# SwiGLU gate and up products with tokens on partitions, weight chunks split whole into rings, and a written order on four engines

## The chip, the core and the metric

The kernel runs on one core of a Trainium2 chip. The engines that matter are TensorE (PE, matrix products), VectorE (DVE), ScalarE (ACT), GpSimd (POOL) and SyncE (SP, which issues the weight transfers). The metric is the device time of the program in microseconds (us). Before the change three runs took 753.84, 753.91 and 754.42 us; the median is 753.91.

## The reference

A hybrid decoder layer on 256 tokens of width 1024, all in float32. Three sub-layers follow each other, each with an RMS norm before and after it: a SwiGLU FFN of width 2816, a mixer (a Mamba-2 branch and a differential-attention branch, merged by gates), and a second SwiGLU FFN. What the change rewrites is the gate and up part of

```python
def swiglu(x, w_gate, w_up, w_down):
    return (jax.nn.silu(x @ w_gate) * (x @ w_up)) @ w_down
```

and the handling of all weights.

## The kernel before

**Split products.** Float32 accuracy comes from three products of reduced operands. Each operand is split into hi, a rounded copy (ACT, `whi`, L167), and lo, the rest (DVE, `wlo`, L168); a product is hi x hi + lo x hi + hi x lo. Activations are split in the same way (L191, L192).

**Chunks.** All weights come from DRAM in 122 chunks of 1 MB, [128 partitions x 2048], loaded by SP into three `raw` buffers. Each chunk is split in two halves of 1024 columns; the halves lie in one pool of 29 buffers (`k4`) that other tiles share. `take` hands a chunk to the products and has the chunks split three ahead (AHEAD). Chunks 0 to 32 belong to the first FFN, 33 to 88 to the mixer, 89 and up to the second FFN.

**The FFN.** The tokens are two blocks of 128. The first 512 columns of gate and of up are done by `mm_nat` (L222): activations stationary, 512 weight columns moving, tokens on partitions; PE turns the result by transposes (`pt_f`, L551). The other 2304 columns of each are done by `mm_w` (L206): weights stationary, chunks of 1024 x 256. For each 128x128 piece of weight, hi moves 512 columns (256 tokens' hi and lo) and lo moves 256. Its result lies with the columns on partitions, which is the form that the down product needs. ACT copies one half of the sum out (L219) and DVE adds the other (L220), then come silu, the product and its split.

**The down product** (`mm_n`, L427) accumulates in four PSUM tiles, two token blocks b by two halves q of 512 columns. The last three chunks are held: block 0 is done for all three, then block 1, first the half q=0 for the three chunks, then q=1. So block 0's norm can run while block 1 is done. `turned` puts block 0's transposes for the next sub-layer (`pu`, L340) among the products of block 1.

**The norms.** After each sub-layer, per block: two square sums on ACT (`jp`, L325), the gain product on DVE (`og`, L411), the power on POOL (`rp`, L330 and L331), the residual on DVE (`h`, L420). For the next norm two square sums (`sq`, L325), the power on POOL (`r`), the scaling (`un`, L373), PE's transposes (`pu`), and the split of the turned result (`u`, L343 and L345). Block 0 goes on unscaled, and its scale comes in later; block 1 is scaled first. `Norm.products` does the first four chunks of the next sub-layer for both blocks, eight products of 12 matmuls; a table says after which product block 1 is turned (after the third, in the mixer and the second FFN).

**The order.** A scheduler sets the order of the instructions on each engine, apart from the stretches in which `own_order` takes the written order for the engines it names: all four at the start and PE alone in the tails of the two kinds of down product, up to the end of the eight products behind them. SP and POOL take their queues in order, transfers too.

Of the kernel before, what the change touches and what calls it, by code (L numbers as in the profile page):

```python
# [24 lines left out]
P = 128  # L25
# [8 lines left out]
K4_BUFS = 29  # L34
K3_BUFS = 3
K2_BUFS = 7
RAW_BUFS = 3
AHEAD = 3
# [5 lines left out]
SSD_US = 1.55  # L44
BREAK, STOP = object(), object()
# [3 lines left out]
def tile_hybrid_layer(ctx: ExitStack, tc: tile.TileContext, x, ffn1_pre_g, ffn1_w_gate, ffn1_w_up,  # L49
# [9 lines left out]

    def k4(shape, name, dt=F32):  # L60
        return sb.tile(shape, dt, tag="k4", name=name, bufs=K4_BUFS)

    def k3(shape, name, dt=F32):
        return sb.tile(shape, dt, tag="k3", name=name, bufs=K3_BUFS)
# [4 lines left out]
    def jk(shape, name):  # L69
        return sb.tile(shape, F32, tag="jk", name=name, bufs=2)  # L70
# [16 lines left out]
    chunks = []  # L87

    def t_chunk(w, k0, c0):
        chunks.append((w[k0:k0 + D, c0:c0 + T].rearrange("(j p) c -> p j c", p=P), [P, KD, T]))  # L90

    def s_chunk(w, k0, c0):
        chunks.append((w[k0:k0 + 512, c0:c0 + 512].rearrange("(j p) c -> p j c", p=P), [P, 4, 512]))

    def n_chunk(w, k0):
        chunks.append((w[k0:k0 + 2 * P, :].rearrange("(j p) c -> p j c", p=P), [P, 2, D]))
# [3 lines left out]

    def ffn_chunks(wg, wu, wd):
        for w in (wg, wu):
            for k0 in (0, 512):
                s_chunk(w[0], k0, 0)
        for j in range(2, FF // T):
            t_chunk(wg[0], 0, j * T)
            t_chunk(wu[0], 0, j * T)
        for j in range(FF // T):
            n_chunk(wd[0], j * T)

    ffn_chunks(ffn1_w_gate, ffn1_w_up, ffn1_w_down)
    for c in range(2):
        for k0 in (0, 512):
            s_chunk(w_in2, k0, V0 + c * 512)
# [9 lines left out]
    for c in range(4):  # L124
        for k0 in (0, 512):
            s_chunk(w_in2, k0, G0 + c * 512)
    for c in range(2):
        for k0 in range(0, 2 * D, 512):
            s_chunk(ssd_w_branch[0], k0, c * 512)
    for c in range(2):  # L130
        for k0 in (0, 512):
            s_chunk(da_w_branch[0], k0, c * 512)
    for c in range(4):
        n_chunk(w_out[0], c * 2 * P)
    ffn_chunks(ffn2_w_gate, ffn2_w_up, ffn2_w_down)

    raws, splits = [], []
    taken = [0]

    def load_to(n):  # L140
        while len(raws) < min(n, len(chunks)):
            i = len(raws)
            src, shape = chunks[i]
            r = sb.tile(shape, F32, tag="raw", name=f"raw{i}", bufs=RAW_BUFS)
            nj = shape[1] // 4 if i == 0 else shape[1] // 2 if i < 4 else shape[1]
            for j in range(0, shape[1], nj):
                nc.sync.dma_start(r[:, j:j + nj, :], src[:, j:j + nj, :])
            raws.append(r)

    def split_steps(ahead=True):  # L150


        i = len(splits)
        load_to(i + 1)
        r, shape = raws[i], chunks[i][1]
        nj = shape[1] // 2
        his, los = [], []
        splits.append((his, los))
        for q in range(2):
            hi = k4([P, nj, shape[2]], f"whi{i}{q}", F32R)  # L160
            lo = k4([P, nj, shape[2]], f"wlo{i}{q}", F32R)
            his.append(hi)
            los.append(lo)
            n = 1 if i == 0 else nj
            for j in range(0, nj, n):
                js = slice(j, j + n)
                nc.scalar.copy(hi[:, js, :], r[:, q * nj + j:q * nj + j + n, :])  # L167
                nc.vector.tensor_sub(lo[:, js, :], r[:, q * nj + j:q * nj + j + n, :], hi[:, js, :].bitcast(F32))  # L168
                yield
        raws[i] = None  # L170
        if ahead:
            load_to(i + 1 + RAW_BUFS)

    def split_to(n):

        while len(splits) < min(n, len(chunks)):
            for _ in split_steps():
                pass

    def take(ahead=AHEAD):  # L180
# [3 lines left out]
        split_to(i + ahead)  # L184
        his, los = splits[i]
        splits[i] = None
        nj = chunks[i][1][1] // 2
        return (lambda j: his[j // nj][:, j % nj, :], lambda j: los[j // nj][:, j % nj, :])
# [17 lines left out]
    def mm_w(dst, name, w, act):  # L206


        (wh, wl), (ah, _, ahl) = w, act
        for m in range(2):  # L210
            acc = pj(f"{name}{m}")
            cs = slice(m * P, (m + 1) * P)
            for j in range(KD):
                if j:
                    nc.tensor.matmul(acc[:, :T], wl(j)[:, cs], ah(j), start=False, stop=False)  # L215
                nc.tensor.matmul(acc, wh(j)[:, cs], ahl(j), start=j == 0, stop=j == KD - 1)  # L216
                if not j:
                    nc.tensor.matmul(acc[:, :T], wl(j)[:, cs], ah(j), start=False, stop=False)
            nc.scalar.copy(dst[:, m, :], acc[:, T:])  # L219
            nc.vector.tensor_tensor(dst[:, m, :], acc[:, :T], dst[:, m, :], ALU.add)  # L220

    def mm_nat(acc, w, act, k0, first, last, late):  # L222
# [7 lines left out]
        for i, ((a, b), j) in enumerate(terms):  # L230
            nc.tensor.matmul(acc, a(k0 + j), b(j), start=first and i == 0, stop=last and i == 11)  # L231
# [43 lines left out]
    load_to(RAW_BUFS)  # L275
# [60 lines left out]
    def turn(b, q, src, g, to, name):  # L336
# [7 lines left out]
        for i in range(4):  # L344
            nc.vector.scalar_tensor_tensor(lo[:, i, :], pu[:, i, :], g(q * 4 + i), hi[:, i, :].bitcast(F32),  # L345
                                           ALU.mult, ALU.subtract)
        return pu

# [73 lines left out]
    def load_gain(v, name):  # L422
        pg = k4([P, D], name)
# [3 lines left out]
    def mm_n(acc, acts, ready, turned, begun=lambda: None):  # L427
# [25 lines left out]
        own_order(PE)  # L453
# [4 lines left out]
        for q in range(2):  # L458
            for i, w in held:
                if q == 1 and i == n - TAIL:  # L460
                    turned()
                one(i, w, ((1, (q,)),))
        split_to(taken[0] + AHEAD)
        ready(1)

    class Norm:
# [3 lines left out]
        def __init__(self, tag, g):  # L470
# [4 lines left out]
            self.left = []  # L475

# [8 lines left out]
        def unit1(self, engs=(nc.vector, nc.vector)):  # L485
            r = rms(1, self.tag)
            self.un = [unit(1, q, r, self.tag, engs[q]) for q in range(2)]

        def turn1(self, q):
            turn(1, q, self.un[q], self.g, in_u(1), self.tag)  # L490

        def products(self, ws, evict, at, turns=((0, 0), (0, 1), (1, 0), (1, 1)), late="u"):
# [4 lines left out]
            for b, i in turns:  # L497
                act = of_block(self.to0 if b == 0 else in_u(1))
                acc = pj(f"pn_{self.tag}{b}{i}")
                for c in range(2):  # L500
                    mm_nat(acc, ws[2 * i + c], act, c * 4, c == 0, c == 1, late if b == 0 else "u")
                    n += 1
                    for f in at.get(n, ()):
                        f()
                if b == 1:
# [3 lines left out]
            free_order()  # L509
# [11 lines left out]
        def rescale(self):  # L521
            set_u(rescaled(self.pus, self.r0, self.g, self.tag, self.dr))
# [7 lines left out]
    def ffn(post_v, tag, norm, ready, turned, then, at, ws=None, **kw):  # L530
# [16 lines left out]
        def back(b):  # L547
            bs = slice(b * P, (b + 1) * P)
            pt_ = bg([P, 4, P], f"pt_{tag}{b}")
            for m in range(4):  # L550
                nc.tensor.transpose(pt_[:, m, :], sgs[b][:, m * P:(m + 1) * P], ident)  # L551
            split(gh[:, :, bs], gl[:, :, bs], pt_)

        norm.products(ws or [take(1) for _ in range(4)], evict,
                      {n: [f if f else lambda: back(0) for f in fs] for n, fs in at.items()}, **kw)
        back(1)
        del sgs
        then()
        for j in range(2, FF // T):
# [633 lines left out]
```

## Time and profile before

| what | us |
|---|---|
| median of three runs | 753.91 |
| profiled execution, its span | 753.1 |
| TensorE busy (share of the span) | 743.7 (99%) |
| VectorE busy | 521.7 (69%) |
| ScalarE busy | 440.1 (58%) |
| weights and other data read from DRAM | 136.17 MB, 182 GB/s over the span |

The profile shows one execution; its own time is the span of 753.1 us, and the median of the runs lies 0.8 us above it. In the page each row has the engine, the line, the tile that is written and those that are read, the shape and the count. A row of the chain of waits has the start, the duration and what was on the chain; consecutive instructions of a kind are one row. A row of the timeline has the start, the duration (of all instructions in it, if there are several), the instruction, and in brackets the idle time ahead of it with what ended it. A row by stretches of time has the stretch, its length, the busy time of PE, PE's weight loads, DVE, ACT and POOL with the number of instructions, the granted clock, the DMA share and GB/s. PE's matmuls are pipelined, and their durations overlap.

### The profile page before, as it was taken

How to read it: one execution, taken by the hardware profiler on the slowest of the kernel's cores; microseconds unless marked ns; L12 is line 12 of the kernel's file. 1: busy time of each engine (PE TensorE's matmuls, PEld its weight loads, DVE VectorE, ACT ScalarE, POOL GpSimd, SP SyncE). 2: the span in 40 equal slices, each digit the busy share in tenths (PEclk: the TensorE clock that was granted, in tenths of full speed). 3: DMA queues.
4: the chain of work that ended last, by engine and by line, in shares of the span. 5: the costliest groups of instructions: out<-in, count | busy, mean ns of one | idle time of the engine just before them, and what ended most of it. 6: DMA issues, size and time to landing. Idle time of an engine off the chain costs nothing.

```text
span 753.1 us, 11054 instructions
## 1 busy us (share of the span) xinstructions
PE 743.7 (99%) x4377; PEld 646.1 (86%) x4377; DVE 521.7 (69%) x792; ACT 440.1 (58%) x737; POOL 38.2 (5%) x72
## 2 busy tenths in 40 slices
PE   8999999999999999999999999999999999999996
PEld 6888888888889999898999788788888888888885
DVE  6686677654577978767778988695684867766612
ACT  7475566643565565858966556784463756565511
POOL 6400000000300000000000000000010000000000
PEclk9999999999999999999999999999999999999999
DMA  8685765587253556565555463467361776555701
GB/s 300 161 265 182 224 224 207 200 286 228 64 166 116 174 163 215 165 210 176 187 168 177 165 219 127 153 224 251 112 225 56 224 224 217 173 173 183 290 1 56
DMA packets 94212, 137.96 MB, mean 183 GB/s; under 512 B 2684, under 2 KB 68304, under 8 KB 94160
## 3 DMA queue, kind: packets, MB, share of 16 engines
q1 hardware_dynamic: 91488, 129.51, 52.5%
q0 software_dynamic: 2368, 7.22, 3.1%
q8 instruction: 34, 0.56, 0.3%
q10 hardware_dynamic: 304, 0.53, 0.2%
q14 instruction: 18, 0.15, 0.1%
HBM read 136.17 MB, written 1.08 MB: 182 GB/s over the span
## 4 chain that ended last, share of the span: by engine, by line
PE 96%; DVE 1%; DMA 1%; POOL 1%; ACT 1%; issue 0%; SPq 0%; DVEq 0%; POOLq 0%
PE acc_f L441 16%; PE pup_f L216 9%; PE pg_f L216 9%; PE pws L231 6%; PE pgt L231 6%; PE pn_f L231 5%; PE pg_f L215 4%; PE pup_f L215 4%; PE acc_mx L441 3%; PE pn_mx L231 3%; PE pwd L231 3%; PE pxs L204 2%; PE pxs L202 2%; PE pxs L201 2%; PE pz L204 2%; PE pz L201 2%
## 5 line engine op out<-in xcount | busy, mean ns | idle before, releaser
L168 DVE TENSOR_TENSOR wlo<-raw,whi 128x1024 fp32r<-128x1024 f32 (+1 forms) x246 | 291.6, 1214 | 56.3 <-ACT whi L167 53.6
L167 ACT CAST whi<-raw 128x1024 fp32r<-128x1024 f32 (+1 forms) x246 | 247.3, 1044 | 59.9 <-PE acc_f L441 21.8
L216 PE MATMUL pg_f<-u_f,whi 128*128 128x512 f32 x288 | 101.2, 396 | 0.0
L216 PE MATMUL pup_f<-u_f,whi 128*128 128x512 f32 x288 | 101.1, 396 | 0.0
L215 PE MATMUL pg_f<-u_f,wlo 128*128 128x256 f32 x252 | 70.5, 280 | 0.0
L215 PE MATMUL pup_f<-u_f,wlo 128*128 128x256 f32 x252 | 70.3, 279 | 0.0
L216 PEld LDWEIGHTS pg_f<-u_f,whi 128*128 128x128 f32 x288 | 52.9, 188 | 9.7
L216 PEld LDWEIGHTS pup_f<-u_f,whi 128*128 128x128 f32 x288 | 52.7, 188 | 9.8
L441 PE MATMUL acc_f<-whi,gh_f 128*128 128x512 f32 x176 | 58.2, 390 | 0.0
L441 PE MATMUL acc_f<-wlo,gh_f 128*128 128x512 f32 x176 | 58.1, 389 | 0.0
L441 PE MATMUL acc_f<-whi,gl_f 128*128 128x512 f32 x176 | 58.1, 389 | 0.0
L215 PEld LDWEIGHTS pg_f<-u_f,wlo 128*128 128x128 f32 x252 | 47.5, 188 | 1.7
L215 PEld LDWEIGHTS pup_f<-u_f,wlo 128*128 128x128 f32 x252 | 47.5, 189 | 1.6
L220 DVE TENSOR_TENSOR su_f<-pup_f,su_f 128x256 f32<-128x256 f32 x36 | 15.2, 423 | 38.7 <-ACT su_f L219 38.7
L441 PEld LDWEIGHTS acc_f<-whi,gl_f 128*128 128x128 f32 x176 | 33.0, 188 | 6.9
L441 PEld LDWEIGHTS acc_f<-wlo,gh_f 128*128 128x128 f32 x176 | 33.0, 188 | 6.8
L441 PEld LDWEIGHTS acc_f<-whi,gh_f 128*128 128x128 f32 x176 | 33.0, 188 | 6.8
L231 PE MATMUL pgt<-whi,u_mx 128*128 128x512 f32 x128 | 34.8, 400 | 0.0
L201 PE MATMUL pz<-u_mx,whi 128*128 128x256 f32 x128 | 32.3, 288 | 0.0
L202 PE MATMUL pz<-u_mx,whi 128*128 128x256 f32 x128 | 31.8, 284 | 0.0
L201 PE MATMUL pxs<-u_mx,whi 128*128 128x256 f32 x128 | 31.7, 285 | 0.0
L202 PE MATMUL pxs<-u_mx,whi 128*128 128x256 f32 x128 | 31.4, 283 | 0.0
(318 smaller groups left out, 1425.9 us busy)
## 6 DMA issues: line engine op xcount, KB each, us to landing
raw<-in_w_in_dram SPq DMA_DIRECT2D x40, 1024.0 KB, 5.4
raw<-in_ffn_w_down_dram SPq DMA_DIRECT2D x22, 1024.0 KB, 5.3
raw<-in_ffn_w_gate_dram SPq DMA_DIRECT2D x20, 1024.0 KB, 5.7
raw<-in_ffn_w_up_dram SPq DMA_DIRECT2D x20, 1024.0 KB, 6.1
raw<-in_ssd_w_branch_dram SPq DMA_DIRECT2D x8, 1024.0 KB, 5.0
acb<-acd POOLq DMA_DIRECT2D x8, 512.0 KB, 4.9
raw<-in_da_w_branch_dram SPq DMA_DIRECT2D x4, 1024.0 KB, 5.1
raw<-in_w_out_dram SPq DMA_DIRECT2D x4, 1024.0 KB, 4.9
```

The source lines that it names most:

```text
L167: nc.scalar.copy(hi[:, js, :], r[:, q * nj + j:q * nj + j + n, :])
L168: nc.vector.tensor_sub(lo[:, js, :], r[:, q * nj + j:q * nj + j + n, :], hi[:, js, :].bitcast(F32))
L201: nc.tensor.matmul(acc[m], wh(j)[:, cs], ah(k0 + j), start=first and j == ks[0], stop=False)
L202: nc.tensor.matmul(acc[m], wh(j)[:, cs], al(k0 + j), start=False, stop=False)
L204: nc.tensor.matmul(acc[m], wl(j)[:, cs], ah(k0 + j), start=False, stop=last and j == ks[-1])
L215: nc.tensor.matmul(acc[:, :T], wl(j)[:, cs], ah(j), start=False, stop=False)
L216: nc.tensor.matmul(acc, wh(j)[:, cs], ahl(j), start=j == 0, stop=j == KD - 1)
L220: nc.vector.tensor_tensor(dst[:, m, :], acc[:, :T], dst[:, m, :], ALU.add)
L231: nc.tensor.matmul(acc, a(k0 + j), b(j), start=first and i == 0, stop=last and i == 11)
L441: nc.tensor.matmul(acc[b][q], x_[:, ts], w_(kt)[:, halves[q]], start=i == 0 and kt == 0 and x_ is ah and w_ is wh, stop=i == n - 1 and kt ...
```

## The change

1. The 2304 columns of gate and of up that `mm_w` did are now done by `mm_nat`, in groups (GROUPS = "hnnnn"): one half group, whose chunks hold 256 gate and 256 up columns, and four groups of 512. Gate, up, silu and product have tokens on partitions; each result of a block is turned by two or four transposes (`turned_back`), four products later (TURN), and split from PSUM. The code has a further form of group ("s") with functions of its own that GROUPS doesn't choose.
2. A chunk is split by one cast and one subtraction of 2048 columns. Hi and lo have rings of three buffers, one more in the FFNs; `raw` has three, two more in the FFNs. The first two chunks of the mixer and of the second FFN are still split in halves, into `k4`, and the first chunks of all in pieces. `k4` and other tiles come from a pool of the stage (first FFN, mixer, second FFN); a new stage's pool takes the space of the one that was closed.
3. PE, ACT, DVE and SP take the written order in the FFNs' products and from the held chunks of a down product to the end of the eight products behind it. In it, `prepare_to` writes the splits: two chunks ahead before the held blocks, the third and a further cast before block 1's post norm (`ready(1)`), the fourth between block 1's square sums and `un` (`unit1`). Block 1 of the held chunks is done chunk by chunk, both halves together, and block 0's transposes come ahead of the last chunk.
4. The mixer's masks (`m3`, `after_m`, `dneg`) lie in the mixer's pool; the gain of the first post norm is loaded earlier; two small tiles move to `k2`.

```diff
-    def mm_w(dst, name, w, act):
...
+MIX_K4 = 20
+FFN_K4 = 11
+RAW_MORE = 2
+SPLIT_BUFS = 3
+SPLIT_MORE = 1
+TURN = 4
...
+    def ring(kind, n, more, name, c, dt=F32):
+        i = rings.get(kind, 0) % (n + more)
+        rings[kind] = rings.get(kind, 0) + 1
+        if i < n or stage[1][1] != FFN_K4 or mixing(c):
+            return sb.tile([P, 2 * D], dt, tag=kind, name=name, bufs=n)
+        return stage[1][0].tile([P, 2 * D], dt, tag=kind, name=name, bufs=more)
...
+    def cast_next():
+        if not todo and begun[0] < len(uses):
+            more_ops()
+        if todo and todo[0].act:
+            todo[0].act()
+            todo[0].act = None
...
+    def prepare_to(n):
+        while prepared[0] < min(n, len(uses)):
+            next_op()
...
-        own_order(PE)
+        own_order(PE, ACT, DVE, SP)
+        prepare_to(taken[0] + 2)
         for q in range(2):
             for i, w in held:
                 one(i, w, ((0, (q,)),))
         ready(0)
-        for q in range(2):
-            for i, w in held:
-                if q == 1 and i == n - TAIL:
-                    turned()
-                one(i, w, ((1, (q,)),))
-        split_to(taken[0] + AHEAD)
+        while held:
+            if len(held) == 1:
+                turned()
+            one(*held.pop(0), ((1, (0, 1)),))
+        prepare_to(taken[0] + 3)
+        cast_next()
         ready(1)
...
         def unit1(self, engs=(nc.vector, nc.vector)):
             r = rms(1, self.tag)
+            prepare_to(taken[0] + 4)
             self.un = [unit(1, q, r, self.tag, engs[q]) for q in range(2)]
...
+        def turned_back(gu_, b, hi, lo):
+            m = gu_.shape[1] // P
             bs = slice(b * P, (b + 1) * P)
+            pt_ = bg([P, m, P], f"pt_{tag}{slot[0]}")
+            for i in range(m):
+                nc.tensor.transpose(pt_[:, i, :], gu_[:, i * P:(i + 1) * P], ident)
+            split(hi[:, :, bs], lo[:, :, bs], pt_)
+
+        def product(acc, w, f, k0, first, last, go_on=False, now=None, then=None):
+            for d in [d for d in due if d[0] <= slot[0]]:
+                due.remove(d)
+                d[1]()
+            mm_nat(acc, w, f, k0, first, last, "w", go_on)
+            if now:
+                now()
+            pace()
+            if then:
+                then()
+            slot[0] += 1
+
+        def two(name, evict_):
+            accs = [pj(f"{name}{b}") for b in range(2)]
+            for c in range(2):
+                w = take(1)
+                for b in range(2):
+                    product(accs[b], w, act_b[b], c * 4, c == 0, c == 1,
+                            then=(lambda: evict_(b, accs[b])) if c else None)
+
+        def plain(name, hi, lo):
+            sg = []
+
+            def gate(b, acc):
+                sg.append(k2([P, 512], f"sg_{name}{b}"))
+                act(sg[b], acc, AF.Silu)
+
+            two(f"pg_{name}", gate)
+            two(f"pu_{name}", lambda b, acc: multiplied(sg[b], acc, b, hi, lo))
...
-    m3 = const.tile([P, 3, P], F32, name="m3")
+    m3 = stage[1][0].tile([P, 3, P], F32, tag="m3", name="m3", bufs=1)
```

The first place is ACT at the seam from the first FFN to the mixer. The names: jp_f11 are the square sums of block 1, u0 and u1 the two halves of block 0's turned result, sq_mx the sums for the next norm, whi a chunk's cast. Before:

```order
L325 ACTIVATE jp_f110_1781,sp_f11_1780<-acc_f110_1342 128x512
L343 ACTIVATE u0_mx_1698<-pu_mx00_1718,cols_a_109 128x128 x4
L343 ACTIVATE u1_mx_1699<-pu_mx01_1731,cols_a_109 128x128 x4
L167 CAST whi360_1841<-raw36_1634 128x1024
L167 CAST whi361_1845<-raw36_1634 128x1024
L325 ACTIVATE jp_f111_1785,sp_f11_1780<-acc_f111_1343 128x512
```

And in the change:

```order
L509 ACTIVATE u0_mx_1386<-pu_mx00_1412,cols_a_112 128x128 x4
L509 ACTIVATE u1_mx_1387<-pu_mx01_1425,cols_a_112 128x128 x4
L491 ACTIVATE sq_mx00_1439,ss_mx0_1438<-h_72 128x512
L491 ACTIVATE sq_mx01_1441,ss_mx0_1438<-h_72 128x512
L254 CAST whi35_1458<-raw35_1312 128x2048
L254 CAST whi36_1464<-raw36_1322 128x2048
L491 ACTIVATE jp_f110_1467,sp_f11_1466<-acc_f110_1062 128x512
L491 ACTIVATE jp_f111_1471,sp_f11_1466<-acc_f111_1063 128x512
```

Block 0's square sums moved behind u, two whole casts stand ahead of jp, and both halves of jp are together.

The second place is ACT where the mixer's eight products end. v0 and v1 are the attention's values (v1 is read from pn_mx11, the last of the eight products), wdt_h is the cast of the weight that PE's next matmuls (pdt) need. Before:

```order
L674 COPY v0_1839<-pn_mx10_1927 128x512
L191 CAST u0_mx_1698<-us_mx0_1948 128x4x128
L191 CAST u1_mx_1699<-us_mx1_1953 128x4x128
L167 CAST whi390_2111<-raw39_1849 128x1024
L191 CAST wdt_h_2004<-wdt_2002 128x256
L167 CAST whi391_2115<-raw39_1849 128x1024
L674 COPY v1_1840<-pn_mx11_1975 128x512
```

And in the change:

```order
L371 CAST u1_mx_1387<-us_mx1_1637 128x4x128
L979 COPY v0_1533<-pn_mx10_1611 128x512
L979 COPY v1_1534<-pn_mx11_1659 128x512
L371 CAST wdt_h_1700<-wdt_1698 128x256
L254 CAST whi39_1787<-raw39_1490 128x2048
```

The cast of wdt moved behind v1.

The third place is ACT at the seam from the mixer to the second FFN (jp_mxp are the mixer's square sums, sq_f2 those of the second FFN's norm), in the change:

```order
L491 ACTIVATE sq_f200_5033,ss_f20_5032<-h_72 128x512
L254 CAST whi91_5052<-raw91_4907 128x2048
L491 ACTIVATE sq_f201_5035,ss_f20_5032<-h_72 128x512
L254 CAST whi92_5059<-raw92_4917 128x2048
L509 ACTIVATE u0_f2_4980<-pu_f200_5006,cols_a_112 128x128 x4
L509 ACTIVATE u1_f2_4981<-pu_f201_5019,cols_a_112 128x128 x4
L491 ACTIVATE jp_mxp10_5062,sp_mxp1_5061<-acc_mx10_4857 128x512
L254 CAST whi93_5209<-raw93_4927 128x2048
L491 ACTIVATE jp_mxp11_5066,sp_mxp1_5061<-acc_mx11_4858 128x512
```

Three whole casts stand among the norms' operations; before, block 0's and block 1's first sums stood ahead of u there, as at the first seam.

413 lines of the change are left out of this document (302 added, 111 removed).

## The prediction

> **What bounds the kernel now.** I read the page first, for who is busy; then PE's waits, for what work could be removed from in front of it; then stretches of the FFN by engine, for the price of one matmul.
>
> ```profile
> span 753.1 us, 11054 instructions
> PE 743.7 (99%) x4377; PEld 646.1 (86%) x4377; DVE 521.7 (69%) x792; ACT 440.1 (58%) x737; POOL 38.2 (5%) x72
> PEclk9999999999999999999999999999999999999999
> PE 96%; DVE 1%; DMA 1%; POOL 1%; ACT 1%; issue 0%; SPq 0%; DVEq 0%; POOLq 0%
> ```
> ```profile
> PE warm L294 <- POOL ident L280: 1.6, 1, 1.6
> PE pn_f L231 <- ACT whi L167: 0.6, 1, 0.6
> PE pu_f L340 <- POOL un_f L373: 0.5, 1, 0.5
> PE pac L739 <- DVE av L735: 0.3, 1, 0.3
> PE py L820 <- DVE E L815: 0.2, 1, 0.2
> ```
>
> The span is 753.1 us, 0.8 under the median of the runs shown (753.91), so a sum made on the span gets 0.8 added. The chain of waits is 96% PE at a full clock, and PE's waits for other engines sum to 3.2 us, nearly all in the first microseconds. So nothing is to be gained by relieving ACT or DVE: two thirds busy, they stand behind PE. What counts is how much PE work the change adds or removes, and whether PE gets waits that it lacks now.
>
> **PE work.** A busy time of pipelined matmuls overlaps itself (the page's mean of 390 ns for a 512-column one); the price is the stretch divided by the count.
>
> ```profile
> 46.66:57.84 11.18, 11.18 (x65) 9.74 (x65) 9.70 (x12) 8.31 (x12) 0.00 (x0) 1.00 0.71 224
> 136.15 55.77 PE acc_f L441 x246
> 582.62 0.44 PE pt_f L551 x4
> 586.75 0.52 PE pt_f L551 x4
> 191.92 0.88 PE pu_mx L340 x8
> ```
>
> The first row is one gate chunk and one up chunk of the old form: 32 pairs of a 512-column and a 256-column matmul, 11.18 us. The change removes 36 such chunks, 18 x 11.18 = 201.2 us. It puts in, for 2304 gate and 2304 up columns (nine groups of 512), two halves of the contraction and two blocks of tokens, 9 x 2 x 2 x 12 = 432 matmuls of 512 columns in each FFN, 864 in all. Both forms stream the same columns; the second row, the down product, gives 55.77/246 = 0.2267 us for a 512-column matmul, so 195.9 us: **-5.3**. But the product now has tokens on partitions and must be turned: 2304/128 x 2 blocks x 2 FFNs = 72 transposes of 128x128. The two rows of four (the FFNs' first columns are turned so already) give 0.48 for four on average (the 0.04 to 0.08 extra is the switch between kinds of matmul), the eight together 0.44 for four. 18 x 0.48 = **+8.6** (7.9 to 9.4). PE's own work grows by 3.3.
>
> The Trainium skill (TensorE: Matmul & The Clock Gate, Part 4) puts a 128x128 transpose at about 275 ns in a kernel's context; by that the 72 would take 19.8 us and the sum would be 11.2 higher. The row of eight in 0.88 speaks against it as a price in a stream.
>
> **Wider splits.** One cast and one subtraction of 2048 columns replace two of 1024. From the rows in the next part, ACT's 512 columns take 0.60 and 1024 about 1.02 (2.05 for two), DVE's 0.69 and 1.22: so by estimate 1.95 and 2.28 for 2048. The total of both engines falls (36 copies and 36 adds of each product go too), behind a saturated PE: 0. What costs is that the first half of a chunk is ready later, and that a norm operation behind a split waits twice as long.
>
> The Trainium skill says so too: Perfetto Trace Analysis, Optimizing Scalar/DVE Operations, has larger operations help where the engine is saturated, and breaking instructions up help where it isn't but makes bubbles on others. With DVE at 69% the second half of that rule applies, and it speaks against this part.
>
> **The seam from the first FFN to the mixer.** While PE does the first three mixer products (of token block 0), block 1 must be normed: two square sums (jp), gain products (og), residual (h), two more sums (sq), un, and PE's next transposes.
>
> ```profile
> 187.87 0.60 ACT L325 ACTIVATE jp_f<-acc_f 128x512 f32<-128x512 f32 x1 [3.39 <-PE acc_f L441]
> 192.60 2.17 ACT L343 ACTIVATE u_mx<-pu_mx,cols_a 128x128 fp32r<-128x128 f32 x8
> 194.60 2.05 ACT L167 CAST whi<-raw 128x1024 fp32r<-128x1024 f32 x2
> 197.00 0.60 ACT L325 ACTIVATE jp_f<-acc_f 128x512 f32<-128x512 f32 x1 [0.35 <-PE pt_cols_b L640]
> 200.80 0.63 ACT L325 ACTIVATE sq_mx<-h 128x512 f32<-128x512 f32 x1
> 202.60 0.69 ACT L676 ACTIVATE v<-pn_mx,r_mx 128x512 f32<-128x512 f32 x1 [1.08 <-POOL r_mx L331]
> ```
> ```profile
> 195.85 1.22 DVE L168 TENSOR_TENSOR wlo<-raw,whi 128x1024 fp32r<-128x1024 f32 x1
> 198.36 0.68 DVE L411 TENSOR_TENSOR og_f<-acc_f,pg_f 128x512 f32<-128x512 f32 x1
> 199.29 1.41 DVE L420 SCALAR_TENSOR_TENSOR h<-og_f,rp_f,h 128x512 f32<-128x512 f32 x2 [0.24 <-POOL rp_f L331]
> 202.60 1.02 DVE L373 TENSOR_SCALAR un_mx<-h,r_mx 128x512 f32<-128x512 f32 x2 [1.89 <-POOL r_mx L331]
> ```
> ```profile
> 197.00 8.22 PE pn_mx L231 x36
> 205.22 0.87 PE pu_mx L340 x8
> ```
>
> Count from 187.87, when block 0's sums are done. Now: the second jp of block 1 starts at +9.1, un ends at +15.8, PE turns it at +17.35: 1.6 of slack. In the change PE reaches the same place at the same time, +17.3 (the 8 transposes only move from 18 to 12 matmuls before the accumulators' end). But ACT's written order is u, two sq of block 0, **two whole casts**, then jp. The transposes start at +5.5, so u runs +5.9 to +8.1, sq to +9.4, the casts to +13.35, jp (both) to +14.5. From the end of the second jp to h it was 1.7 (197.60 to 199.29), less now with og waiting only for jp: h +15.7 to +17.1, sq to +17.9; r from sq's end to un was 1.2, and DVE has a whole subtraction (2.28) written between h and un: +17.1 to +19.4. So the first un, half of 1.02 long, is there at +19.9 against +17.3: a stall of **2.5** (1.0 to 3.0: without the subtraction it is 1.5 to 2). A gain is excluded, since PE waits for nothing there now. Late next is v's scaling on ACT, which PE doesn't need before the attention.
>
> **The opening of the mixer.** After its eight products PE takes pdt, from a small weight wdt.
>
> ```profile
> 20.16 0.44 POOL L643 MEMSET m<- 128x384 f32 x1
> 20.67 2.28 POOL L645 TENSOR_SCALAR_AFFINE_SELECT m<-m 128x128 f32<-128x128 f32 x2
> 23.67 0.63 POOL L657 TENSOR_SCALAR_AFFINE_SELECT dneg<-dneg 128x128 f32<-128x128 f32 x2
> 203.29 1.00 POOL L682 DMA_DIRECT2D wdt<-in_w_in_dram  x1
> wdt<-in_w_in_dram POOLq DMA_DIRECT2D x1, 128.0 KB, 3.2
> 219.96 0.12 PE pdt L692
> ```
>
> The masks are made at 20 us now (20.16 to 24.30). In the change they lie in the mixer's pool, whose space is the FFN's: their first write waits for the last PE use of the seam's first two chunks, the end of product 6. POOL goes in order, so wdt's load comes behind 2.4 (without the first select's long 2.28) to 4.1 us of mask work, then 3.2 to land and about 0.4 to cast: +6.0 to +7.7 after product 6, where PE has two products, 24 x 0.2267 = 5.4. Apart from that, ACT now has v's second half, which needs product 8, ahead of the cast: 0.1 + 0.69 + 0.3 = 1.1 after PE is free at the least. Stall 0.6 to 2.3 by the one and 1.1 by the other: **1.7** (1.0 to 2.5).
>
> **Ring of three.** The split chunk i now needs the buffer of chunk i-3. In the mixer's down product chunk 88 gets its buffer when chunk 85 is done, and that is the moment when the three held chunks start.
>
> ```profile
> 545.34 0.59 ACT L191 CAST mh<-pmg 128x512 fp32r<-128x512 f32 x1
> 545.81 2.97 ACT L167 CAST whi<-raw 128x1024 fp32r<-128x1024 f32 x3
> 545.16 12.27 PE acc_mx L441 x54
> ```
>
> Now its cast runs between 542.5 and 546, long before. In the change: 0.1 + 1.95 + 2.28 = 4.3 after the start, needed after 14 matmuls (12 of two chunks and two of its own), 3.2: **+1.2** (0 to 2).
>
> **The seam to the second FFN.** Here ACT has, by order, a whole cast after the first sq and another after the second, both behind ring waits, then u, jp, a third whole cast, and the other jp; DVE has a subtraction between the two og. From the end of block 0: casts to +5.4 and +8.0, u to +10.1, jp to +10.7, cast to +12.6, jp to +13.2, the subtraction to +14.9, og to +15.6, h to +17.0, sq to +17.7, un's first half at +19.4, against +17.3: **+2.3** (1.0 to 3.3).
>
> **The end.**
>
> ```profile
> 742.84 0.60 ACT L325 ACTIVATE jp_f<-acc_f 128x512 f32<-128x512 f32 x1 [2.83 <-PE acc_f L441]
> 746.92 0.60 ACT L325 ACTIVATE jp_f<-acc_f 128x512 f32<-128x512 f32 x1 [3.39 <-PE acc_f L441]
> ```
>
> The half of block 1 that ends first has its jp 4.1 us before the end now; in the change both halves end together and ACT does two in a row: **+0.5** (0 to 0.8).
>
> The steady FFN loop gets nothing: at 5.4 us a chunk its 4.3 of split work lie ahead by more than two chunks, and the DMA share of 0.71 in the row of 11.18 becomes 0.74. The start issues the same. The sum: -5.3 + 8.6 + 2.5 + 1.7 + 1.2 + 2.3 + 0.5 = +11.5, so 764.6 of span, **765.4** of time. The lower bounds give 753.9 - 5.3 + 7.9 + 1.0 + 1.0 + 0 + 1.0 + 0 = 759.5, the upper ones 753.9 - 5.3 + 9.4 + 3.0 + 2.5 + 2.0 + 3.3 + 0.8 = 769.6: the forecast's own range.
>
> **The rivals.**
> B, the order is covered: the casts written before jp are done earlier (chunks and buffers free sooner than I count), so that jp comes as now and the opening waits little. Only PE's 3.3 and the end's 0.5 are left: 757.7. For it: 1.6 of slack now. Against: ACT cannot start those casts before u, which waits for PE.
> C, not slower: the turning costs PE only its columns. At the rate of the 512-column rows, 128 take 0.057; 72 then cost 4.1, net -1.2, and with the waits covered as in B and the end's 0.5 that is 753.2; it decides from under 0.074 a transpose (5.3/72), and with the lowest waits too it would be slower. A product interval 1% shorter would add 2.0: 751. For it: the equal column count. Against: the rows of four and eight, 0.11 each.
> D, the mixer stalls: with rings of three for its 56 chunks and whole splits, ten chunks that lose 0.5 to 1 us each add 5 to 10: 770 to 775. For it: DVE is the fullest engine behind PE and the splits are in a free order there. Against: its split work per chunk, 4.3 over two engines, is less than the 5.4 of the shortest chunk.
> E, turning at the latency of a transpose: the row below has a median of 273 ns; 72 x 0.273 is 19.7, 11.1 more than I take: 776.5. The Trainium skill (TensorE: Matmul & The Clock Gate, Part 4) names such a time, 275 ns.
>
> ```profile
> L551 PE MATMUL pt_f<-ident,sg_f1b x8: 272/273/327, 31.2 to 35.8; 128*128 128x128 f32 x8
> ```
>
> **Chances and range.** Forecast 0.58, B 0.17, C 0.08, D 0.15, E 0.02. From 755 to 771 leaves out C, half of D and E, 0.17. What a measurement of this kernel can tell is about 0.2%, 1.5 us: faster (under 752.4) 0.07, from C and what I don't see; same (to 755.4) 0.07, C's rest and B's edge; slower 0.86.
>
> **What would show it.** Gate and up matmuls at 0.227 apart and transposes in fours of 0.44 to 0.52 confirm PE's terms. PE waits of 1 to 3 us before the transposes of un at both seams, with a whole cast right ahead of jp on ACT, confirm the seams; pdt behind the wdt cast on ACT, the opening; a wait for the subtraction of chunk 88 after 14 held matmuls, the ring. No such waits, and a span near 757, is B. Waits for splits spread over the mixer are D. The forecast is wrong outright if PE's total in the FFNs falls.

## The result, and the profile after

The change makes the kernel slower: 777.18 us, median of four runs (776.99 to 778.96), against 754.16 (753.84 to 754.56) for the kernel before. The ratio is 1.031, 95% interval 1.0296 to 1.0325. The forecast was 765.4 with a range to 771: the direction is right, the size is half of what happened. The profiled execution has a span of 775.5 us, 22.4 more than before, where the sum of the forecast gave 11.5.

The page of the changed kernel, its span, its engines and the share of each in the chain that ended last:

```profile
span 775.5 us, 10252 instructions
PE 759.1 (98%) x4161; PEld 640.7 (83%) x4161; DVE 487.8 (63%) x610; ACT 401.4 (52%) x555; POOL 42.8 (6%) x72
PE 88%; ACT 5%; DVE 2%; issue 2%; POOL 2%; DMA 1%; SPq 0%; DVEq 0%; ACTq 0%; POOLq 0%
```

DVE and ACT lost 34 and 39 us of work, as the wider splits should bring, and the time did not follow. PE is busy 759.1 us in place of 743.7, with 216 instructions fewer. What is new ahead of PE stands in its waits (engine, line and tile that waited, what it waited for, total us, times, longest):

```profile
PE pu_mx L506 <- DVE un_mx L542: 2.6, 1, 2.6
PE pu_f L506 <- DVE un_f L542: 2.0, 1, 2.0
PE warm L460 <- POOL ident L446: 1.6, 1, 1.6
PE pdt L999 <- ACT wdt_h L371: 1.0, 1, 1.0
PE pn_mx L395 <- ACT v L981: 0.8, 1, 0.8
PE pto L1263 <- DVE o L1257: 0.6, 1, 0.6
```

Five of the six are new (the third was there before), and the first, second and fourth are the two seams and the opening of the mixer, nearly as forecast. The five sum to 7.0 us. So two thirds of the 22.4 are not waits: PE itself takes longer. The chain shows where. First the changed kernel, then the kernel before, both in the first FFN's down product, whose matmuls the change leaves alone:

```profile
79.90 11.19 PE pu_f L395 x48
91.09 5.61 PE pg_f L395 x24
143.91 46.29 PE acc_f L610 x200
144.14 5.22 PE acc_f L610 x23
149.36 16.33 PE acc_f L610 x70
```
```profile
139.78 50.32 PE acc_f L441 x222
```

Before, a 512-column matmul came every 50.32/222 = 0.2267 us. After, the new gate and up products take 11.19/48 = 0.2331, and the down product 46.29/200 = 0.2315. Inside it are two rates: 23 matmuls at 5.22/23 = 0.2270 and the next 70 at 16.33/70 = 0.2333. The fast ones use the weight chunk in the fourth place of the ring, the one that the FFN adds and that lies in the stage's pool; the slow ones use the three ring buffers proper. Over the whole kernel 1728 matmuls of 512 columns take 232.7 ns from start to start, and 440 take 227 to 229. Two rates that alternate chunk by chunk within microseconds are not the clock: it is granted in full over this whole stretch (1.00 from 100 to 190 us, in the first row of the table by stretches under e1). Over the run it is 0.993, against 0.999 before; where the 0.993 comes from is told there too.

### The profile page after: what moved, and what is told of

Its sections match the earlier page's. It is cut to its first block, busy times and chain, and to the rows that moved or that the text cites. A ratio compares the mean times of both kernels' runs of the same rounds, so it can differ in the third digit from the quotient of the medians.

```text
span 775.5 us, 10252 instructions
## 1 busy us (share of the span) xinstructions
PE 759.1 (98%) x4161; PEld 640.7 (83%) x4161; DVE 487.8 (63%) x610; ACT 401.4 (52%) x555; POOL 42.8 (6%) x72
## 4 chain that ended last, share of the span: by engine, by line
PE 88%; ACT 5%; DVE 2%; issue 2%; POOL 2%; DMA 1%; SPq 0%; DVEq 0%; ACTq 0%; POOLq 0%
PE acc_f L610 15%; PE pu_f L395 12%; PE pg_f L395 11%; PE pws L395 5%; PE pn_f L395 4%; PE pgt L395 4%; PE ph_f L395 3%; PE pwd L395 3%; ACT whi L254 2%; PE pxs L382 2%; PE pxs L384 2%; PE pxs L381 2%; PE pz L381 2%; PE pz L382 2%; PE acc_mx L610 2%
## 5 line engine op out<-in xcount | busy, mean ns | idle before, releaser
L261 DVE TENSOR_TENSOR wlo<-raw,whi 128x2048 fp32r<-128x2048 f32 (+2 forms) x132 | 280.4, 2132 | 161.9 <-ACT whi L254 160.5
L254 ACT CAST whi<-raw 128x2048 fp32r<-128x2048 f32 (+2 forms) x132 | 233.3, 1777 | 196.9 <-PE pu_f L395 48.9
L395 PE MATMUL pg_f<-whi,u_f 128*128 128x512 f32 x256 | 65.6, 398 | 0.0
L395 PE MATMUL pu_f<-whi,u_f 128*128 128x512 f32 x256 | 65.0, 395 | 0.0
L395 PEld LDWEIGHTS pu_f<-whi,u_f 128*128 128x128 f32 x256 | 48.0, 188 | 11.6
L395 PEld LDWEIGHTS pg_f<-whi,u_f 128*128 128x128 f32 x256 | 46.9, 188 | 9.6
L395 PE MATMUL pu_f<-wlo,u_f 128*128 128x512 f32 x128 | 35.1, 395 | 0.0
L395 PE MATMUL pg_f<-wlo,u_f 128*128 128x512 f32 x128 | 34.7, 392 | 0.0
L395 PEld LDWEIGHTS pu_f<-wlo,u_f 128*128 128x128 f32 x128 | 24.0, 188 | 5.8
L395 PEld LDWEIGHTS pg_f<-wlo,u_f 128*128 128x128 f32 x128 | 24.0, 188 | 5.4
```

The costliest lines, as they stand in the source:

```text
L254: i = nc.scalar.copy(got["hi"](j, step), src()[:, j:j + step, :])
L261: nc.vector.tensor_sub(got["lo"](j, step), src()[:, j:j + step, :], got["hi"](j, step).bitcast(F32))
```

## The experiments

The lead theory after the result (**A**, for address) was that the slow rate hangs on where the weights lie in SBUF, the core's own memory. In the layout of the built program the ring buffers start at 32 modulo 256 bytes in each partition, since small tiles (square sums, powers) lie ahead of them; the activations, and all tiles of the stage's pool, start at 160. In the kernel before, weights and activations both start at 160. The rival (**R**) was that the ring's order of reuse, or the clock, sets the rate.

**e1, the rings moved by 128 bytes.** Two pads of 128 bytes, one ahead of the rings and one behind them, so that what lies behind both moves by 256 bytes and keeps its start modulo 256.

```diff
+    sb.tile([P, 32], F32, tag="pad", name="pad", bufs=1)
     prepare_to(1)
+    sb.tile([P, 32], F32, tag="pad2", name="pad2", bufs=1)
```

> The changed kernel with 128 unused bytes per partition ahead of the split rings and 128 behind them: the rings' start goes from 32 to 160 modulo 256 bytes, all other tiles on PE's moving side stay, and the instructions and their order are the same. Theory A (where a weight tile starts in SBUF sets the rate of the 512-column matmuls that move it): the 1728 of them that move ring tiles go from 232.7 ns to about 227 ns, 1728 x 5.7 ns = 9.9 us less, 767.3 us. Rival R (the slower matmuls come with the order written out, the whole-chunk splits or the transposes): within 1 us of 777.2.

Measured: 768.94 us (767.55 to 769.45), ratio to before 1.0199 [1.0182, 1.0216], where A had 767.3: 8.2 less than the change, median against median. The profiled execution, the fastest of the four, has a span of 765.9, 9.6 less than that of the change; the other three have 767.1 to 767.7 at a granted clock of 0.995 to 0.997. The chain of e1 at the same places:

```profile
79.75 10.88 PE pu_f L395 x48
90.62 5.44 PE pg_f L395 x24
96.07 0.44 PE pt_f L740 x4
142.36 47.85 PE acc_f L610 x211
```

10.88/48 = 0.2267 and 47.85/211 = 0.2268: the rate of before is back in every product. R falls for this rate, as the rings' order and reuse are untouched and the clock was full in both down products.

But not all of the 9.6 is the rate. Here is the changed kernel by stretches of time: the down product above, then what follows the two seams.

```profile
100.00:190.00 90.00, 90.00 (x399) 73.06 (x398) 44.03 (x28) 37.41 (x31) 0.00 (x0) 1.00 0.50 164
211.00:215.00 4.00, 3.63 (x14) 3.25 (x15) 2.20 (x9) 2.48 (x9) 2.67 (x5) 0.57 1.10 282
586.00:590.50 4.50, 4.31 (x16) 3.69 (x17) 2.72 (x10) 2.17 (x8) 0.28 (x1) 0.62 0.01 2
```

A mean of 0.57 over 4.0 us and of 0.62 over 4.5 is half the clock for 3.4 us in each. In e1's profiled execution the clock behind both seams is 1.00. PE there, first the change, then e1:

```profile
211.37 1.97 PE pu_mx L506 x8
587.73 6.69 PE pn_f L395 x24
```
```profile
208.79 1.09 PE pu_mx L506 x8
582.54 5.49 PE pn_f L395 x24
```

From start to start the eight transposes and the 24 products behind them take 8.00 us in the change and 6.41 in e1 at the first seam, 8.07 and 6.43 at the second: 3.2 together, of which the rings' rate can be at most 0.1 at each seam (24 x 6 ns). So about 3 of the 9.6 are the halved clock, in these two executions. It follows the waits of PE for `un` there, but these alone don't decide it: e1's are longer (2.8 and 2.3 us), and its profiled execution has none, while e2 has the same two stretches as the change. Nor do all runs show what it costs: the fourth run of the change, granted 0.997, has a span of 775.3, only 0.2 under the profiled one, and there is no trace of it.

**e2, e3 and e4, everything moved.** If it were the place itself (128 bytes off some border), a pad ahead of all tiles would cure the changed kernel in another way (e2) and harm the kernel before (e3); e4 asks whether a smaller border counts.

```diff
+    const.tile([P, 32], F32, name="pad")
     stage_a = const.tile([P, P], F32, name="stage_a")
```

That is e2 on the changed kernel; e3 has the same line in the kernel before, and e4 has 8 floats for the 32 there.

> The changed kernel with 128 unused bytes ahead of everything: rings go to 160 modulo 256, but the stage pools and the activations go from 160 to 32. Theory A: ring matmuls faster as in the run with the rings moved (-9.9), the 440 that move tiles of the stage pools slower (+2.5): 769.8 us, and in the trace the two groups change places. Rival R: 777.

> The kernel before with 128 unused bytes ahead of everything: all tiles go from 160 to 32 modulo 256. Theory A: the 1391 matmuls of 512 columns that move weights go from 227 to 232.7 ns: +7.9, about 762 us. Rival R: 754.

> The kernel before with 32 unused bytes ahead of everything: all tiles at 192 modulo 256, so at 0 modulo 64. Theory A doesn't say which starts are fast apart from 160 and 32; if 64-byte borders count, the gate and up pairs (350 ns for 768 columns, 340 by the rate of the others) could gain up to 576 x 10 ns = 5.8 us: 748. If only the distance from a 128-byte border in a 256-byte line counts: 754. Rival R: 754.

Measured, one run each: e2 777.88, e3 754.25, e4 753.72; the kernel before ran at 753.62 to 754.43 beside them. Both forecasts of A on the place itself missed. The chain of e2, in the same down product:

```profile
144.61 45.61 PE acc_f L611 x197
```

45.61/197 = 0.2315, as in the change without the pad. In e2 the rings now start at 160, but the activations moved too, to 32: their distance is 128 as before. Its 440 fast matmuls have both operands at 32, those of before both at 160. So neither place is slow by itself, and what fits is the distance between the starts of the moving and the stationary operand.

**e5, e6 and e7, other distances.** In the kernel before, a pad of 8, 16 or 24 floats ahead of the pool that holds the weights sets the distance from the activations to 32, 64 and 96 bytes.

```diff
+    sb.tile([P, 16], F32, tag="pad", name="pad", bufs=1)
     raw_u = [k4([P, 4, 2, P], f"raw_u{q}", F32R) for q in range(2)]
```

> The kernel before with 32 unused bytes between the activations u (still at 160 modulo 256) and the pool of the weights (192): products that pair u with weights have their two operands 32 bytes apart modulo 256, the down product keeps 0. Theory A2 (what counts is the distance between the starts of the moving and the stationary operand modulo 256: 0 is fast, 128 slow) says nothing of 32 yet. If 32 is as bad as 128, the 480 matmuls of 512 columns that move weights over u (pn, pgt) take 5.7 ns more: +2.7, 756.7. If it is better than 0 for the products that move u, up to 1867 x 7 ns (120 to 113) for the 256-column ones and 576 x 10 ns for the gate and up pairs come off. Rival: the distance doesn't matter but for 128: 754.

> The same with 64 bytes. Theory A2: 754 if only 128 is slow, 756.7 if every distance apart from 0 is, less if the products that move u gain.

> The same with 96 bytes. Theory A2: 754, or 756.7 if the penalty comes with any distance.

Measured, one run each: 756.26, 749.56 and 754.36, with the kernel before at 753.87 to 754.41. The chain of before, e5, e6 and e7 in that order; pn_mx are 512 weight columns moving over an activation, pbc 256 activation columns moving over a weight:

```profile
211.78 8.18 PE pn_mx L231 x36
235.51 0.96 PE pbc L204 x8
```
```profile
212.44 8.40 PE pn_mx L231 x36
236.40 0.95 PE pbc L204 x8
```
```profile
211.81 8.26 PE pn_mx L231 x36
235.35 0.91 PE pbc L204 x8
```
```profile
211.68 8.40 PE pn_mx L231 x36
238.42 0.94 PE pbc L204 x8
```

Divided by the counts (the row for 128 is from the changed kernel, pu_f above and its pbc row of 0.95 for eight):

| distance of the starts, bytes | 512 columns, ns | 256 columns, ns |
|---|---|---|
| 0 (before, e1) | 227 | 120 |
| 32 (e5) | 233 | 119 |
| 64 (e6) | 229 | 114 |
| 96 (e7) | 233 | 118 |
| 128 (change) | 233 | 119 |

The distance is that of the weights from the activations. In the column of 512 the weights move, so the moving operand starts that far ahead of the stationary one; in the column of 256 the activations move, and it starts that far behind. So 64 in one column and 64 in the other are not the same case. In e1 the rings lie 256 modulo 512 bytes from the activations and are fast, so the pattern repeats at 256 there. The 114 is one row of eight: over the mixer's 256-column matmuls of e6 the trace has about three quarters at 113 to 114 and a quarter at 117 to 118. At 64 the 512-column matmuls lose 2 ns but those of 256 columns gain 6: from before to e6 the 256-column products of the mixer gain 7.1 us over some 1340 intervals, gate and up lose 1.2, the other 512-column products 1.0. That is -4.9 worked out, -4.6 measured. The first FFN's down product in e6 is a control: both its operands lie in the pool that moved, and its rate stays at 227 ns.

**e9, the same kernel as e6 in five rounds.**

> The kernel before with the weights' pool 64 bytes further from the activations u modulo 256, again, now timed in five rounds: 749.6 us, 4.5 under the kernel before, if the one time seen holds; 754 if it was chance.

Measured: 750.29 (749.58 to 750.8) against 754.22, ratio 0.9945 [0.9925, 0.9966]. One line with a pad of 64 bytes beats both kernels by a little; it is the fastest version found here.

**e8, the seams undone.** On top of e1: at the seams no whole cast stands ahead of block 1's square sums on ACT, and no whole subtraction ahead of `un` on DVE; the third chunk is split before block 0's transposes.

```diff
+        free_order()
         own_order(PE, ACT, DVE, SP)
...
         while held:
             if len(held) == 1:
+                prepare_to(taken[0] + 3)
                 turned()
             one(*held.pop(0), ((1, (0, 1)),))
-        prepare_to(taken[0] + 3)
-        cast_next()
         ready(1)
...
             r = rms(1, self.tag)
-            prepare_to(taken[0] + 4)
             self.un = [unit(1, q, r, self.tag, engs[q]) for q in range(2)]
+            prepare_to(taken[0] + 4)
```

The first power of the mixer and of the second FFN (`self.r0`) also moves from behind the transposes (`block0`) to the norm's start. `free_order` is needed because the mixer had taken the written order for PE alone (L1374) shortly before, and a second call inside does nothing: so in the change the scheduler, not the written order, still places ACT's and DVE's work at the second seam.

> The changed kernel with the rings moved as before, and with the two seams' order changed: block 0's square sums come ahead of the transposes, one whole cast follows them, and no further split is written until block 1's un is issued; at the second seam the written order is really taken by ACT and DVE. Theory S (the splits written among the norm's operations hold back jp and un): both stalls ahead of un's transposes, 2.8 and 2.3 us in the run with the rings moved, are gone or under 0.5: 768.9 - 5 = 764. Rival (the norm's chain is late by itself, or the weights become late in place of un): stalls of 2 us or more stay at or right behind the seams, 767 to 769.

Measured: 761.8 (761.3 to 762.0), ratio 1.01 [1.0083, 1.0116], span 760.1, 5.8 under e1. Both waits for `un` are gone from PE's list, as the theory that the order of the splits causes them (S) has it. ACT and DVE at the first seam (start, duration, idle time ahead), the changed kernel first, then e8:

```profile
197.15 2.17 ACT L509 ACTIVATE u_mx<-pu_mx,cols_a 128x128 fp32r<-128x128 f32 x8 [5.29 <-PE pu_mx L506]
...
200.38 3.75 ACT L254 CAST whi<-raw 128x2048 fp32r<-128x2048 f32 x2
203.98 0.64 ACT L491 ACTIVATE jp_f<-acc_f 128x512 f32<-128x512 f32 x1
```
```profile
207.70 2.29 DVE L261 TENSOR_TENSOR wlo<-raw,whi 128x2048 fp32r<-128x2048 f32 x1
210.83 0.89 DVE L542 TENSOR_SCALAR un_mx<-h,r_mx 128x512 f32<-128x512 f32 x2 [0.84 <-POOL r_mx L497]
```
```profile
197.48 0.60 ACT L491 ACTIVATE jp_f<-acc_f 128x512 f32<-128x512 f32 x1 [0.84 <-PE acc_f L610]
```
```profile
203.21 0.88 DVE L542 TENSOR_SCALAR un_mx<-h,r_mx 128x512 f32<-128x512 f32 x2 [1.89 <-POOL r_mx L497]
205.93 0.87 PE pu_mx L506 x8
```

In the change the first `jp` of block 1 stands right behind two whole casts of 3.75 us; in e8 it waits only for PE. From its start to `un` the change takes 6.9 us, e8 5.7. Of this difference 1.15 us is the first step of the power on POOL, which `un` waits for. First the changed kernel, then e8:

```profile
208.70 1.45 POOL L496 TENSOR_SCALAR r_mx<-ss_mx 128x1 f32<-128x1 f32 x1 [2.37 <-ACT sq_mx L491]
```
```profile
202.23 0.30 POOL L496 TENSOR_SCALAR r_mx<-ss_mx 128x1 f32<-128x1 f32 x1 [2.45 <-ACT sq_mx L491]
```

The same sum of two columns takes 0.30 us alone and 1.45 under DVE's whole subtraction (207.70 to 209.99), and ends at 210.15, just behind it. In e8 `un` is ready at 204.1, and PE turns it at 205.93.

**e10, the opening.** On top of e8: v's tiles get a place of their own outside the stage's pool (to make room the mixer's pool has 18 `k4` for 20 and `raw` one buffer less), and wdt's load and cast are written behind product 7, ahead of v's last copy.

```diff
-    vt = [k4([P, 2, 512], f"v{b}") for b in range(2)]
+    vt = [sb.tile([P, 2, 512], F32, tag="v", name=f"v{b}", bufs=2) for b in range(2)]
...
-                  {3: [norm.turns1], 5: [norm.settle, norm.rescale]})
+                  {3: [norm.turns1], 5: [norm.settle, norm.rescale], 7: [load_wdt]})
```

> The kernel with the rings moved and the seams reordered (761.8), and with the mixer's opening changed: the attention's values v lie outside the stage's pool, so that their scaling no longer waits for product 6; wdt's cast is written ahead of the last copy of v; to make room the FFNs have one more raw buffer rather than two, and the mixer 18 shared buffers rather than 20. The masks stay behind product 6. Theory O (v's wait for the pool and the place of wdt's cast on ACT make the two stalls, 1.0 and 1.2 us): 761.8 - 1.9 = 759.9, no wait over 0.3 ahead of pdt. Rival M (the masks on POOL hold wdt's load back, whatever ACT does): the first stall goes, the second stays at 1 or more, 760.8.

Measured: 761.33 (760.25 to 766.76), ratio 1.0107 [1.0073, 1.0141], span 759.7, so 0.4 under e8, less than its own runs differ. The times don't tell the two theories apart; the waits do. The opening of the changed kernel, POOL and ACT:

```profile
222.58 0.42 POOL L948 MEMSET m<- 128x384 f32 x1 [8.87 <-PE pn_mx L395]
225.31 0.97 POOL L989 DMA_DIRECT2D wdt<-in_w_in_dram  x1 [0.33 <-DVE us_mx L561]
```
```profile
222.60 1.26 ACT L981 ACTIVATE v<-pn_mx,r_mx 128x512 f32<-128x512 f32 x2 [6.12 <-issue]
228.76 1.06 ACT L979 COPY v<-pn_mx 128x512 f32<-128x512 f32 x2
229.72 0.41 ACT L371 CAST wdt_h<-wdt 128x256 fp32r<-128x256 f32 x1
```

The opening of e10, ACT, POOL and the wait of PE:

```profile
208.92 0.75 ACT L984 ACTIVATE v<-pn_mx,r_mx 128x512 f32<-128x512 f32 x1
222.02 0.41 ACT L371 CAST wdt_h<-wdt 128x256 fp32r<-128x256 f32 x1 [1.58 <-DMA wdt<-in_w_in_dram]
```
```profile
218.82 0.97 POOL L990 DMA_DIRECT2D wdt<-in_w_in_dram  x1
```
```profile
PE pdt L1006 <- ACT wdt_h L371: 1.3, 1, 1.3
```

In the change the masks and v's scaling begin at the same moment, 222.6, when the seam's chunks come free. v's own place takes away the wait of 0.8 (its scaling runs at 208.92). The wait for wdt stays at 1.3: its cast no longer stands behind v, and waits for the load, which POOL issues only when the masks are done (in the change it waits a further 0.33 for DVE). So the masks in the stage's pool stand in its way, as the rival M has it, and the written place of the cast alone brings nothing. To move the masks out as well was not tried, so what they cost is argued from this order and not measured.

**e11, e8 with the rings 64 bytes off** (pads of 48 and 16 floats in place of 32 and 32), to join the two gains.

> The kernel with the seams reordered (761.8), and the rings 64 bytes off the stationary tiles modulo 256 rather than 0. By the intervals seen in the kernel before with 64 bytes: the 512-column matmuls 227 to 229 ns (2171 x 2 ns = +4.3), the mixer's 256-column ones 120 to 113 ns (1339 x 7 ns = -9.4): 756.7. Rival (the gain of the 256-column ones belongs to the older layout in halves): 766.

Measured: 761.46 (760.97 to 761.95), ratio 1.0094 [1.006, 1.0128], span 759.3; the 756.7 expected was missed, and the time is within what e8 itself spans. The interval of 512 columns rose to 229 ns in nearly all products (from start to start they take about 3.5 us more in the trace than in e8, 2.7 of it in gate, up and the FFNs' down products), and the 256-column products gain only 4 to 5: about half of them stay at 117 to 119 ns, where in e6 a quarter did, at the same distance modulo 256. So this distance alone does not set the interval of 256 columns, and what else does stays open.

## Why the prediction was right and wrong

**The step that failed is the price of a 512-column matmul**: 55.77/246 = 0.2267 us, read in the down product of before, put on all of the change's products, and taken as unchanged for products that the change leaves alone. The runs show 0.227 for operands whose starts lie 0 modulo 256 bytes apart, as in before and e1, and 0.2327 for the rings of the change. The change takes the weights out of the pool that gave them the distance 0 and puts them behind small tiles, 128 bytes off. The sum was short by 10.9 us of span, and e1 takes away 9.6. Of these, 3.8 lie in gate, up and their transposes (209.9 us from start to start in the change, 206.1 in e1) and 2.5 in the FFNs' down products (122.9 and 120.4); 3.2 lie behind the two seams, nearly all of it the halved clock; the rest, the mixer's products against the start and the waits, comes to 0.1. So the rings' place is worth 6 to 7 us. **The second thing missing is the clock**: the sum has PE at a full clock throughout, as before had it, and no term for the two stretches at half, about 3 us in this execution. The down products and the mixer were not priced at all, since the change leaves their matmuls as they were. With the rings at the right distance the remainder is 12.8 (765.9 less 753.1), against 11.5; by the medians it is 14.9 (768.94 less 754.02). That it comes so near is in part luck: chunk 88, the products and the transposes cost 1.5 less than forecast, the seams (5.8 by e8), small waits and what I can't place about 3 more.

**Products and transposes: right in size.** Gate, up and transposes together (starts to starts, all their matmuls) take 203.3 us before and 206.1 in e1: +2.8, forecast +3.3. In the change itself it is +6.6. Four transposes take 0.44 in the chain of e1, the lower end of what was taken (0.48). Rival E is wrong although its 776.5 is nearest to the time: the transposes of the change last 272 ns each but follow each other four in 0.44. So the 275 ns of the Trainium skill (TensorE: Matmul & The Clock Gate, Part 4) agree as a duration, and are no price in a stream.

**The two seams: right.** Forecast 2.5 and 2.3 (the steps written out give 19.9 less 17.3, 2.6, and 19.4 less 17.3, 2.1), waits measured 2.6 and 2.0. At the first seam `jp` came at +12.8 (forecast +13.35) and `un` began at +19.7 (forecast +19.4); at the second `jp` came at +9.4 (+10.7), and `un` began at +18.9. A size in it came from another source than I gave: the subtraction ahead of `un` was to delay it as work in DVE's queue, but the row of 1.45 tells that it also holds up the power on POOL. The Trainium skill (SBUF — State Buffer, Who interferes with whom) has a VectorE instruction with two SBUF inputs contend with a GpSimd instruction that reads SBUF, the later one blocked; the rows of 1.45 and 0.30 agree. e8 shows the cause by taking it away: -5.8. The waits themselves exclude rival B. The rule that the prediction quotes from the Trainium skill (Perfetto Trace Analysis, Optimizing Scalar/DVE Operations) is borne out in one half: here larger operations on unsaturated engines come with 5.1 us of bubbles (idle time) on another, by the two waits of e1 that e8 removes:

```profile
PE pu_mx L506 <- DVE un_mx L542: 2.8, 1, 2.8
PE pu_f L506 <- DVE un_f L542: 2.3, 1, 2.3
```

That breaking them up would help no run here shows, since e8 leaves them whole and moves them.

**The opening: 1.7 forecast, 1.8 measured, in another way, so the agreement is luck.** The wait for wdt is 1.0; the other 0.8 is v, whose tiles lie in the stage's pool like the masks, so ACT's scaling, and behind it the PSUM that product 7 needs, waits for product 6. I saw this of the masks and did not ask it of the other tiles of that pool. Both bounds for wdt that I gave (POOL's masks, v's copy) exist; in e10 the one by the masks stays.

**Chunk 88: forecast 1.2, measured 0.2** (PE's acc_mx waits for wlo). The held chunks start at 557.57. The cast of chunk 88 began 0.6 ahead of that, at 556.99, where the forecast has 0.1 behind it: a group of four transposes that was left out lies between chunk 85 and the held chunks, and the cast needs only the hi buffer. So the subtraction ended 3.7 after their start (forecast 4.3), and PE asked for it at 3.5 (forecast 3.2), after 15 matmuls of 0.232.

**The end: forecast 0.5, measured 0.46.** When the accumulators are done, ACT has one `jp` left in before and two in the change. It began 6.18 us ahead of the span's end in before, and the first of the two 6.64 ahead in the change:

```profile
768.86 0.60 ACT L491 ACTIVATE jp_f<-acc_f 128x512 f32<-128x512 f32 x1 [6.85 <-PE acc_f L610]
769.45 0.59 ACT L491 ACTIVATE jp_f<-acc_f 128x512 f32<-128x512 f32 x1
```

**Rival D** (the mixer stalls): its waits are single ones of 0.2 to 0.6, about 1 us in all, not 5 to 10. **Rival C**: wrong by the transposes' price, and the product interval that it hoped to find 1% shorter is nearly 3% longer.

Of the 22.4 us, then: 9.6 what e1 takes away (6 to 7 the rings' place, about 3 the halved clock), 5.8 the seams (e8), and 7.0 what is left in e8: 2.8 of PE's own work, 1.9 of the opening, 0.5 of the end, about 1 of small waits, and 0.8 that I can't place.

## What to carry to other kernels

When a change moves a matmul's operands to other buffers, the interval measured before is no longer a given: compare the starts of the moving and the stationary tile, and look for two rates within one stretch of like matmuls, which no clock explains. A padding tile of 64 or 128 bytes is a cheap experiment for it, in both directions. Before a difference of two runs is put down to one cause, read the granted clock by stretches of time and at the seams too: here its mean of 0.993 hid two stretches at half. Where large operations replace small ones on engines that stand behind PE, look at the short chain of norm operations in which PE waits for them, and write the large ones behind that chain; and when tiles move to a pool whose space comes free late, ask of every tile in it who writes it first.

## What the runs showed that I had not expected

The time from one matmul of the split operands (fp32r in the profile) to the next depends on the distance between the starts of its two SBUF operands modulo 256 bytes, by 227 to 233 ns for 512 columns and by 114 to 120 for 256, with the lowest of the five rows not the same for both (0 and 64), and with more than this distance behind the figures of 256 (e6 and e11). For 0 and 128 several runs show it; each other distance rests on one kernel or two. A common shift of both by 32 or 128 bytes changes nothing (e3, e4). The granted clock was 0.993 in three of the four runs of the change and in e2, and 0.995 to 0.999 in e1, with the same work. In the traces of the change and of e2 this is half the clock for two stretches of 3.4 us behind the seams; what brings them, the waits of 2.0 and 2.6 us or something else, was not tested. What in the machine makes the distance count stays open.
